# Projecting the recurrence values with 512 tokens moving, and turning them with VectorE blocks, in a hybrid decoder layer

## The chip, the cores and the metric

The kernel runs on one core of one Trainium2 chip. The metric is the device time of one execution in microseconds; a profiled execution also has a span, from its first to its last instruction, and a trace of every instruction and transfer. The engines are called PE or TensorE (matmul), PEld (its weight load), DVE or VectorE, ACT or ScalarE, POOL or GpSimd, and SP or SyncE, which here issues nearly all DMAs.

## The reference, cut to what matters

A decoder layer on 2048 tokens of width 1024 in float32. Its input projection feeds two groups of heads side by side: four recurrent heads (HGRN2) of width 128, and eight attention heads over a window of 128 tokens. The change is about `hi`, the values of the recurrent heads.

```python
u = rmsnorm(h, norm_mix_w[l])
proj = u @ w_in[l]
hq, hf, hi, hg, att = jnp.split(proj, [...], axis=-1)
f = lb + (1.0 - lb) * jax.nn.sigmoid(hf)
log_f, k_hg = jnp.log(f), 1.0 - f
q_hg = hq * (HG_DK ** -0.5)
v_hg = hi.reshape(B, S, HG_HEADS, HG_DV)
o_hg = hgrn2_chunkwise(q_hg, k_hg, v_hg, log_f)   # S_t = diag(f_t) S_{t-1} + k_t v_t^T,  o_t = S_t^T q_t
o_hg = rmsnorm(o_hg, hg_norm_w[l]) * silu(hg)
o_att = sliding_window_attention_with_sinks(...)
h = h + concatenate([o_hg, o_att]) @ w_out[l]
v = rmsnorm(h, norm_ffn_w[l])
h = h + (silu(causal_depthwise_conv(v @ w_gate[l])) * (v @ w_up[l])) @ w_down[l]
return rmsnorm(h, final_norm_w)
```

## The kernel before

The tokens are done in two halves of 1024. In each half there is a mixing stage (all head projections, the recurrence and the attention), then the output projection, gate and up projections, and the down projection. The normalized input X of a half lies in SBUF with the features on the partitions, as 8 pairs of tiles XH and XL, each 128 x 1024. Each float32 product is made of three matmuls in a faster format, from a high and a low part of either side (hi and lo of a weight, made by `prep` at L199 and L200; XH and XL of the input): XH x hi, XL x hi, XH x lo.

Most projections go through `unit` (L218): for one head, the weight tile of 128 x 128 is the stationary operand and 512 tokens move, so the result lies with the head's 128 columns on the partitions and the tokens along the row, in two PSUM tiles of 128 x 512, one for each 512 tokens: 8 x 3 x 2 = 48 matmuls. PSUM has eight banks of this size: four of kind mm, which the units use in turn, two of kind hg and two of kind at.

The values are needed the other way round, with tokens on the partitions. `project_v` (L670 to L686) therefore makes them with X as the stationary operand and the weights of two heads, 256 columns, moving: for each of the 8 groups of 128 tokens one mm bank `pvv`, filled by 24 matmuls of 256 columns (L681 to L683) and emptied by two ScalarE activations (L685), one for each head, which multiply by the token's norm `rs` as they copy. It is called twice in a half, once for heads 0 and 1 and once for heads 2 and 3. The values are read by `pu` (L614, with the transposed keys Kn, for the state's updates) and by `po` (L634, with the score tile ST).

What has a tile with tokens and columns exchanged elsewhere uses one of two ways: TensorE transposes through PSUM (`pkn` at L607 for the keys, `ppt`, `pot`), or the helper `turned` (L335): one VectorE instruction STREAM_TRANSPOSE (L338) exchanges rows and columns within each block of 32 x 32 into a tile `turn`, and sixteen DMAs on SyncE's queue (L341) carry the blocks, 32 KB a time and from SBUF to SBUF, to their places in the destination. The attention probabilities of head pairs 0 to 2 (`pt`, from `sc`) and the output of recurrent heads 0 to 2 (`hg`, from `on`) go that way. The tiles of tag pp, three buffers, serve both `turn` and the attention's `qx` (the split queries, L401 to L404) and `po` (the masked probabilities, L453).

The attention of one pair of heads j has these steps: `qa` projects the queries; `sc` makes, for each of two groups of 512 tokens, the scores `psc` (L414), the softmax on VectorE and ScalarE (maximum at L426, exponentials at L436, scaling at L441), and the turning into `pt`; `pv` and `pw` multiply with the values: `poT` (L471), from `pt` and from `po`. A recurrent head has the steps f, q (projections), l (seven levels of short matmuls `plev`, L558 and L572, with VectorE multiplications between them), s (keys transposed, `pu`, the states `SS`) and p (`po`, L634 and L639, and the norm). The string ORDER gives the order in which the steps are written out; the framework's scheduler then places every instruction in its engine's queue, mixing steps where their data allow, and each engine executes its queue in that order.

Of the kernel before, what the change touches and what calls it, by code (L numbers as in the profile page):

```python
# [36 lines left out]
            ("P7", "S3", "T3"), ("P2", "A12", "B21"), ("P4", "A22", "T4")]  # L37
AFTER = {2: 'po'}
UP_AFTER = 'T2'
ORDER = ("f0 q0 l0 qa0 v0 sc0 s0 p0 f1 q1 pv0 pw0 l1 qa1 sc1 f2 s1 p1 q2 pv1 pw1 l2 qa2 v1 sc2 f3 s2 p2 q3 pv2 "  # L40
         "pw2 l3 qa3 sc3 s3 p3 pv3 pw3 g0 g1 m4 m5 m6 g2 m0 m1 g3 m7 m2 m3").split()
LEVELS = [1, 2, 4, 8, 16, 32, 64]
NEG = -1.0e30
UT = 7
# [1 line left out]
VB = 2  # L46
TURNED_PAIRS = 3
TURNED_HEADS = 3


@with_exitstack
def hymba_layer(ctx: ExitStack, tc: tile.TileContext, a: dict, out: bass.AP, rows_out: bass.AP):
# [282 lines left out]
    def turned(p, tag, bufs, src, dst):  # L335

        t = p.tile([P, 4, 8, 32], F32, tag=tag, name="turn", bufs=bufs)
        nc.vector.transpose(t, src.rearrange("p n (c j) -> p c n j", j=32))  # L338
        for a in range(4):
            for c in range(4):  # L340
                nc.sync.dma_start(dst[32 * c:32 * c + 32, a], t[32 * a:32 * a + 32, c])  # L341

    def rows(kv):
        return slice(kv * HD, (kv + 1) * HD)
# [38 lines left out]
    def attend(hf, j, X, invb, KS, V, VD, mix, p):  # L383
# [9 lines left out]
        for g in range(NB):  # L393
            sc = p.tile([P, 2, 4, P], F32, tag="sc", name="sc", bufs=2)
            gs = slice(g * 512, (g + 1) * 512)
            for kv in range(2):
                r, other = rows(kv), rows(1 - kv)

                qx = p.tile([P, 2, 512], F32R, tag="pp", name="qx", bufs=3)
                qh, ql = qx[:, 0], qx[:, 1]  # L400
                nc.scalar.copy(qh[r], qT[r, gs])  # L401
                nc.scalar.copy(qh[other], qT[r, gs])
                nc.vector.tensor_tensor(ql[r], qT[r, gs], qh[r].bitcast(F32), op=ALU.subtract)
                nc.scalar.copy(ql[other], ql[r].bitcast(F32))  # L404
                for i0 in (0, 2):
                    pb = ps("at", "psc")
                    first = hf == 0 and g == 0 and i0 == 0
                    for i in range(2):
                        n = g * 4 + i0 + i
                        w0 = 1 if first and i == 0 else 0  # L410
                        o = pb[:, i * 256 + w0 * P:(i + 1) * 256]
                        ks = slice((n + w0) * P, (n + 2) * P)
                        for t, qx in enumerate((qh, ql)):
                            nc.tensor.matmul(o, qx[:, (i0 + i) * P:(i0 + i + 1) * P], KS[:, kv, ks],  # L414
                                             start=t == 0, stop=t == 1)
                    pv = pb.rearrange("p (i w k) -> p i w k", i=2, w=2)
                    dst = sc[:, kv, i0:i0 + 2]
                    if first:
                        nc.vector.memset(dst[:, 0], NEG)
                        nc.scalar.copy(dst[:, 1], pv[:, 1, 0])  # L420
                    else:
                        nc.scalar.copy(dst, pv[:, :, 0])
                    nc.vector.copy_predicated(
                        dst, C.own.bitcast(U32).unsqueeze(1).to_broadcast([P, 2, P]), pv[:, :, 1])
            m = p.tile([P, 2, 4], F32, tag="mx", name="m", bufs=2)
            nc.vector.tensor_reduce(m.rearrange("p a b -> p (a b)"),  # L426
                                    sc.rearrange("p a b c -> p (a b) c"), axis=AX.X, op=ALU.max)
# [4 lines left out]
            nc.vector.tensor_scalar(m, m, -1.0, None, op0=ALU.mult)
            den = p.tile([P, 2, 4], F32, tag="den", name="den", bufs=2)
            for kv in range(2):
                for i in range(4):
                    nc.scalar.activation(sc[:, kv, i], sc[:, kv, i], AF.Exp, bias=m[:, kv, i:i + 1],  # L436
                                         accum_out=den[:, kv, i:i + 1])
# [3 lines left out]
            nc.vector.tensor_tensor(sc, sc, den.unsqueeze(3).to_broadcast([P, 2, 4, P]), op=ALU.mult)  # L441
            if j < TURNED_PAIRS:
                pt = p.tile([P, 4, 8, 32], F32, tag="sc", name="pt", bufs=2)
                turned(p, "pp", 3, sc.rearrange("p a b c -> p (a b) c"), pt)
                sc = pt
            scs.append(sc)
        yield
# [37 lines left out]
    def hgrn(hf, h, X, invb, vs, WG, gates, mix, p, fu=None):  # L485
# [112 lines left out]
        v = vs[h]  # L598

        kept = TT if hf + 1 < NH else TT - 1  # L600
        Kn = p.tile([P, TT, P], F32, tag="t4", name="Kn", bufs=2)
        for b in range(NB):
            pk = ps("hg", "pkn")
            n = min(4, kept - 4 * b)
            for i in range(n):
                c = slice((b * 4 + i) * P, (b * 4 + i + 1) * P)
                nc.tensor.transpose(pk[:, i * P:(i + 1) * P], K[:, c], ident)  # L607
            nc.scalar.copy(Kn[:, 4 * b:4 * b + n].rearrange("p a b -> p (a b)"), pk[:, 0:n * P])
        SS = p.tile([P, TT, P], F32, tag="SS", name="SS", bufs=1)
        for b in range(NB):  # L610
            pu = ps("hg", "pu")
            for c in range(4 * b, min(4 * b + 4, kept)):
                i = c % 4
                marks["pu"] = nc.tensor.matmul(pu[:, i * P:(i + 1) * P], Kn[:, c], v[:, c], start=True, stop=True)  # L614
            for c in range(4 * b, min(4 * b + 4, kept)):
                i = c % 4
                if hf == 0 and c == 0:
                    nc.vector.tensor_copy(SS[:, 0], pu[:, 0:P])
                    continue
# [9 lines left out]
        for b in range(NB):  # L629
            at = [po[b][:, i * P:(i + 1) * P] for i in range(4)]  # L630
            empty = hf == 0 and b == 0
            for i in range(4):
                for k in range(2):
                    marks["po"] = nc.tensor.matmul(at[i][rows(k)], ST[:, k, 4 * b + i], v[:, 4 * b + i],  # L634
                                                   start=i == 0, stop=empty and i == 0, skip_group_check=True)
            for i in range(4):
                c = 4 * b + i
# [11 lines left out]
            mix[h] = g  # L649
        nc.vector.tensor_tensor(on, on, rs.unsqueeze(2).to_broadcast([P, TT, P]), op=ALU.mult)  # L650
        if h < TURNED_HEADS:
            turned(p, "t4", 2, on, q.rearrange("p (a c q) -> p a c q", a=4, c=TT))
        for b, bs in halves() if h >= TURNED_HEADS else ():
            pt = ps("hg", "pot")
            for i in range(4):
# [11 lines left out]
            nc.vector.tensor_copy(state[:, h], SS[:, TT - 1])  # L667
        yield

    def project_v(hf, pr, X, rs, p):  # L670

        v = [p.tile([P, TT, P], F32, tag="v", name="v", bufs=VB) for _ in range(2)]
        parts = [prep(a["w_v"][pr, s]) for s in range(2)]
        for tt in range(TT):
            o = ps("mm", "pvv")
            t = slice(tt * P, (tt + 1) * P)
            for kt in range(KT):
                hi, lo = parts[kt // 4]
                xh, xl = X[kt]
                c = slice((kt % 4) * 256, (kt % 4 + 1) * 256)  # L680
                nc.tensor.matmul(o[:, 0:256], xh[:, t], hi[:, c], start=kt == 0, stop=False)  # L681
                nc.tensor.matmul(o[:, 0:256], xl[:, t], hi[:, c], start=False, stop=False)  # L682
                nc.tensor.matmul(o[:, 0:256], xh[:, t], lo[:, c], start=False, stop=kt == KT - 1)  # L683
            for i in range(2):
                nc.scalar.activation(v[i][:, tt], o[:, i * P:(i + 1) * P], AF.Identity, scale=rs[:, tt:tt + 1])  # L685
# [468 lines left out]
    for hf in range(NH):  # L1154
        X, kv, invb, rs, f0 = nxt
        with ExitStack() as st:
# [7 lines left out]
            for name in ORDER:  # L1164
# [7 lines left out]
                elif stage == "w":  # L1172
                    WG[n] = prep(a["w_g"][n])
                elif stage == "v":
                    vs += project_v(hf, n, X, rs, p)
                else:
                    M[n] = split(mix[n], C.hgw if n < TURNED_HEADS else None)
            for n in (7, 3):
# [8 lines left out]
def _layout(i):  # L1187
# [3 lines left out]
    def cols(w, idx):  # L1191
# [10 lines left out]
    rows = [ar(P) + h * P for h in range(4)]  # L1202
    rows += [512 + np.concatenate([j * HD + ar(HD), (j + 4) * HD + ar(HD)]) for j in range(4)]
    w_out = i["w_out"][0][np.concatenate(rows)]
    w_v = np.stack([cols(w_in, 1024 + pr * 256 + ar(256)).reshape(P, 2, D).transpose(1, 0, 2) for pr in range(2)])
    conv = np.concatenate([i["conv_w"][0], i["conv_b"]], 0)
    d = {
        "xT": x.T.reshape(KT, P, S),
# [1 line left out]
        "norm_mix_w": i["norm_mix_w"][0].reshape(KT, P).T,  # L1210
        "w_q": np.stack([cols(w_in, h * P + ar(P)) for h in range(4)]),
        "w_f": np.stack([cols(w_in, 512 + h * P + ar(P)) for h in range(4)]),
        "w_v": w_v,
        "w_g": np.stack([cols(w_in, 1536 + h * P + ar(P)) for h in range(4)]),
        "w_att": np.stack([cols(w_in, c) for c in att]),
        "b_attn": np.stack([b[c - att0] for c in att], 1),
# [37 lines left out]
```

## Time and profile before

| what | value |
|---|---|
| runs, median of three | 2129.17 us (2129.09 to 2129.24) |
| the profiled execution | 2129.44 us |
| its span | 2127.7 us |
| mean granted TensorE clock | 0.999 |
| PE busy | 2113.7 us (99%) |
| VectorE busy | 1632.4 us (77%) |
| ScalarE busy | 1050.0 us (49%) |
| mixing stage of half 0, roughly | 45 to 346 us |
| mixing stage of half 1, roughly | 1085 to 1400 us |

A row of the timeline reads: start, duration, engine, line, operation, tile written, tile read, count, and in brackets the idle time before it with what ended it. A row of a group ends in busy time, mean ns of one, and the idle time before its members. A row of a stretch has its bounds, its length, then for each engine the busy time and the count, the granted clock, the DMA share and GB/s. Matmuls overlap: the duration of one is longer than the distance between the starts of two.

### The profile page before, as it was taken

What the parts mean: (1) busy time and instruction counts of PE and PEld (TensorE: products, weight loads), DVE (VectorE), ACT (ScalarE), POOL (GpSimd) and SP (SyncE); (2) the same over time, 40 slices, a digit from 0 to 9 for tenths busy, and PEclk for the clock granted to TensorE, in tenths of its full rate; (3) what the DMA queues carried; (4) which work ended last, traced back from release to release, by engine and by line L of the source; (5) the groups of instructions that cost most, each with busy time, mean ns of one, the idle gap of its engine ahead of it and who ended that gap; (6) DMA issues with size and microseconds to landing.
All of it is one profiled execution on the core that took longest, in us unless ns stands there. A gap on an engine that the chain in (4) does not pass through costs nothing.

```text
span 2127.7 us, 30275 instructions
## 1 busy us (share of the span) xinstructions
PE 2113.7 (99%) x11575; PEld 1763.0 (83%) x11575; DVE 1632.4 (77%) x2427; ACT 1050.0 (49%) x1855; POOL 16.9 (1%) x43
## 2 busy tenths in 40 slices
PE   8999999999999999999999999999999999999998
PEld 6988888888888888888889898888888888888887
DVE  6587786798887878785865776867988788887765
ACT  5455645564444445335635456555544444453353
POOL 2000000000000000000000000000000000000000
PEclk9999999999999999999999999999999999999999
DMA  4121213413232335964641212242223323259644
GB/s 162 42 59 45 68 52 102 136 59 121 91 124 92 98 116 168 379 235 150 216 143 40 61 38 64 60 146 97 80 99 103 110 90 124 94 194 403 228 149 134
DMA packets 105810, 264.34 MB, mean 124 GB/s; under 512 B 15808, under 2 KB 28608, under 8 KB 105664
## 3 DMA queue, kind: packets, MB, share of 16 engines
q1 hardware_dynamic: 105232, 262.14, 36.6%
q8 instruction: 91, 1.49, 0.3%
q14 instruction: 55, 0.45, 0.1%
q10 hardware_dynamic: 432, 0.27, 0.0%
HBM read 195.56 MB, written 57.34 MB: 119 GB/s over the span
## 4 chain that ended last, share of the span: by engine, by line
PE 97%; DVE 2%; DMA 1%; ACT 0%; issue 0%; SPq 0%; ACTq 0%; DVEq 0%
PE X L818 7%; PE X L816 7%; PE X L817 7%; PE pop L218 7%; PE hq L218 4%; PE q L218 4%; PE g L218 4%; PE f L218 4%; PE Y L817 4%; PE Y L818 4%; PE Y L816 4%; PE pdx L1004 3%; PE pdx L1003 3%; PE pdx L1005 3%; PE pdy L1004 3%; PE pdy L1003 3%
## 5 line engine op out<-in xcount | busy, mean ns | idle before, releaser
L689 ACT CAST whi<-raw 128x1024 fp32r<-128x1024 f32 x88 | 92.7, 1053 | 115.1 <-PE X L817 73.1
L816 PE MATMUL X<-T,whi 128*128 128x512 f32 x352 | 136.9, 389 | 0.0
L817 PE MATMUL X<-T,whi 128*128 128x512 f32 x352 | 136.9, 389 | 0.0
L818 PE MATMUL X<-T,wlo 128*128 128x512 f32 x352 | 136.9, 389 | 0.0
L887 DVE SCALAR_TENSOR_TENSOR y<-ga,cw,y 128x1024 f32<-128x1024 f32 x88 | 112.5, 1279 | 25.9 <-ACT y L885 25.9
L822 ACT COPY u<-X 128x512 f32<-128x512 f32 x88 | 51.5, 585 | 122.8 <-PE X L818 122.6
L690 DVE TENSOR_TENSOR wlo<-raw,whi 128x1024 fp32r<-128x1024 f32 x88 | 107.2, 1218 | 4.4 <-ACT whi L689 4.4
L199 ACT CAST whi<-raw 128x1024 fp32r<-128x1024 f32 x58 | 60.6, 1050 | 89.9 <-PE pop L218 36.7
L690 DVE TENSOR_TENSOR xld<-raw,xhd 128x1024 fp32r<-128x1024 f32 x72 | 80.9, 1131 | 18.3 <-ACT xhd L689 18.2
L689 ACT CAST xhd<-raw 128x1024 fp32r<-128x1024 f32 x72 | 70.0, 978 | 37.6 <-DMA raw<-act0T 12.0
L218 PE MATMUL pop<-XL,whi 128*128 128x512 f32 x256 | 82.8, 390 | 0.0
L218 PE MATMUL pop<-XH,wlo 128*128 128x512 f32 x256 | 82.6, 390 | 0.0
L218 PE MATMUL pop<-XH,whi 128*128 128x512 f32 x256 | 82.5, 391 | 0.0
L200 DVE TENSOR_TENSOR wlo<-raw,whi 128x1024 fp32r<-128x1024 f32 x58 | 70.5, 1217 | 10.4 <-ACT whi L199 10.1
L818 PEld LDWEIGHTS X<-T,wlo 128*128 128x128 f32 x352 | 66.1, 188 | 13.8
L817 PEld LDWEIGHTS X<-T,whi 128*128 128x128 f32 x352 | 66.1, 188 | 13.7
L816 PEld LDWEIGHTS X<-T,whi 128*128 128x128 f32 x352 | 66.0, 188 | 13.7
L682 PE MATMUL pvv<-whi,XL 128*128 128x256 f32 x256 | 72.7, 285 | 0.0
L681 PE MATMUL pvv<-whi,XH 128*128 128x256 f32 x256 | 72.6, 285 | 0.0
L683 PE MATMUL pvv<-wlo,XH 128*128 128x256 f32 x256 | 72.4, 287 | 0.0
L818 PE MATMUL X<-B,wlo 128*128 128x512 f32 x176 | 68.7, 390 | 0.8 <-DVE wlo L690 0.8
L817 PE MATMUL X<-T,Sh 128*128 128x512 f32 x176 | 68.6, 390 | 0.5 <-DVE T L690 0.5
(388 smaller groups left out, 6287.9 us busy)
## 6 DMA issues: line engine op xcount, KB each, us to landing
wr<-in_w_down SPq DMA_DIRECT2D x90, 512.0 KB, 5.6
raw<-in_w_gate SPq DMA_DIRECT2D x44, 512.0 KB, 3.6
raw<-in_w_up SPq DMA_DIRECT2D x44, 512.0 KB, 3.6
raw<-act0T SPq DMA_DIRECT2D x20, 512.0 KB, 5.6
raw<-act1T SPq DMA_DIRECT2D x20, 512.0 KB, 5.9
act0B<-y SPq DMA_DIRECT2D x33, 256.0 KB, 2.4
act1B<-y SPq DMA_DIRECT2D x33, 256.0 KB, 2.4
raw<-in_w_out SPq DMA_DIRECT2D x16, 512.0 KB, 3.7
```

Source lines behind the costliest of these rows:

```text
L218: nc.tensor.matmul(o[b], w, x[:, bs], start=f, stop=l)
L681: nc.tensor.matmul(o[:, 0:256], xh[:, t], hi[:, c], start=kt == 0, stop=False)
L682: nc.tensor.matmul(o[:, 0:256], xl[:, t], hi[:, c], start=False, stop=False)
L683: nc.tensor.matmul(o[:, 0:256], xh[:, t], lo[:, c], start=False, stop=kt == KT - 1)
L689: nc.scalar.copy(h, src)
L690: return (eng or nc.vector).tensor_tensor(l, src, h.bitcast(F32), op=ALU.subtract)
L816: nc.tensor.matmul(o, wh[:, ws], xh, start=i == 0 and not more, stop=False, skip_group_check=more)
L817: nc.tensor.matmul(o, wh[:, ws], xl, start=False, stop=False, skip_group_check=more)
L818: nc.tensor.matmul(o, wl[:, ws], xh, start=False, stop=i == 3, skip_group_check=more)
L887: nc.vector.scalar_tensor_tensor(y, g[:, w:w + HALF], C.cw[:, ft, w:w + 1], y, op0=ALU.mult, op1=ALU.add)
L1003: nc.tensor.matmul(o, wh[:, i, c], ah[:, i, cols], start=f, stop=False, skip_group_check=more)
L1004: nc.tensor.matmul(o, wh[:, i, c], al[:, i, cols], start=False, stop=False, skip_group_check=more)
```

## The change

The values of each head are projected by `unit`, with the weights stationary and 512 tokens moving, into two PSUM tiles `vT0` and `vT1`. The helper `turned`, which now takes a list of sources, transposes them in blocks of 32 x 32, with one VectorE instruction for each PSUM tile, into `turn`, and its sixteen DMAs carry the blocks into the tile `v`, now laid out as 4 strips of 32 columns for each group of 128 tokens. ScalarE then multiplies each group of 128 tokens by its norm in place. The step v stands for one head instead of two; in ORDER v0 v1 stand where v0 stood, and v2 v3 where v1 stood. TURNED_KEYS is 0, so the keys go through `pkn` as before. The DMAs in `turned` are the same as before, from `turn` to the destination.

```diff
-ORDER = ("f0 q0 l0 qa0 v0 sc0 s0 p0 f1 q1 pv0 pw0 l1 qa1 sc1 f2 s1 p1 q2 pv1 pw1 l2 qa2 v1 sc2 f3 s2 p2 q3 pv2 "
+ORDER = ("f0 q0 l0 qa0 v0 v1 sc0 s0 p0 f1 q1 pv0 pw0 l1 qa1 sc1 f2 s1 p1 q2 pv1 pw1 l2 qa2 v2 v3 sc2 f3 s2 p2 ...
+TURNED_KEYS = 0
 def turned(p, tag, bufs, src, dst):
     t = p.tile([P, 4, 8, 32], F32, tag=tag, name="turn", bufs=bufs)
-    nc.vector.transpose(t, src.rearrange("p n (c j) -> p c n j", j=32))
+    for i, s in enumerate(src):
+        n = 8 // len(src)
+        nc.vector.transpose(t[:, :, i * n:(i + 1) * n], s.rearrange("p (n c j) -> p c n j", n=n, j=32))
     for a in range(4):
         for c in range(4):
             nc.sync.dma_start(dst[32 * c:32 * c + 32, a], t[32 * a:32 * a + 32, c])
...
-                marks["pu"] = nc.tensor.matmul(pu[:, i * P:(i + 1) * P], Kn[:, c], v[:, c], start=True, stop=True)
+                marks["pu"] = nc.tensor.matmul(pu[:, i * P:(i + 1) * P], Kn[:, :, c] if h < TURNED_KEYS else Kn[:, c], v[:, :, c], start=True, stop=True)
...
-                    marks["po"] = nc.tensor.matmul(at[i][rows(k)], ST[:, k, 4 * b + i], v[:, 4 * b + i],
+                    marks["po"] = nc.tensor.matmul(at[i][rows(k)], ST[:, k, 4 * b + i], v[:, :, 4 * b + i],
...
-    def project_v(hf, pr, X, rs, p):
-        v = [p.tile([P, TT, P], F32, tag="v", name="v", bufs=VB) for _ in range(2)]
-        parts = [prep(a["w_v"][pr, s]) for s in range(2)]
-        for tt in range(TT):
-            o = ps("mm", "pvv")
-            t = slice(tt * P, (tt + 1) * P)
-            for kt in range(KT):
-                ...
-                nc.tensor.matmul(o[:, 0:256], xh[:, t], hi[:, c], start=kt == 0, stop=False)
-                nc.tensor.matmul(o[:, 0:256], xl[:, t], hi[:, c], start=False, stop=False)
-                nc.tensor.matmul(o[:, 0:256], xh[:, t], lo[:, c], start=False, stop=kt == KT - 1)
-            for i in range(2):
-                nc.scalar.activation(v[i][:, tt], o[:, i * P:(i + 1) * P], AF.Identity, scale=rs[:, tt:tt + 1])
+    def project_v(h, X, rs, p):
+        o = unit(a["w_v"][h], X, "vT")
+        v = p.tile([P, 4, TT, 32], F32, tag="v", name="v", bufs=VB)
+        turned(p, "pp", 3, o, v)
+        for c in range(TT):
+            nc.scalar.activation(v[:, :, c], v[:, :, c], AF.Identity, scale=rs[:, c:c + 1])
         return v
```

The scheduler's order moves with it. Three places matter for what follows, all in half 0. On TensorE, the end of the second values pass before the change: the last pvv matmuls, the first two poT of the second group of pair 1 (they read pt, which the sixteen DMAs fill), a level plev, the rest of poT, and the first matmuls of f of head 3.

```order
L681 MATMUL pvv<-whi,XH 128x256
L682 MATMUL pvv<-whi,XL 128x256
L471 MATMUL poT<-pt,V 64x128 [waits DMAHW4_49,DMAHW5_49,DMAHW3_49,DMAHW6_49,DMAHW2_49,DMAHW7_49,DMAHW1_49,DMAHW0_49]
L471 MATMUL poT<-pt,V 64x128
L558 MATMUL plev<-Q,G 64x2x32 [waits DVE_49,Activation_49]
L558 MATMUL plev<-Q,G 64x2x32 x7
L683 MATMUL pvv<-wlo,XH 128x256
L414 MATMUL psc<-KS,qx 128x128 [waits Activation_49]
L471 MATMUL poT<-po,VD 64x128 [waits DVE_49]
```

The same place after the change, from the last level of 16 on, which now follows the end of the last vT unit and the first group's poT: three levels, the transposes of K (pkn) and poT of the second group stand behind each other, and f of head 3 comes after them.

```order
L560 MATMUL plev<-Q,G 64x2x32 x7
L574 MATMUL plev<-Q,K 32x32 [waits DVE_49]
L574 MATMUL plev<-Q,K 32x32 x15
L574 MATMUL plev<-Q,K 64x64 [waits DVE_49,PE_49]
L574 MATMUL plev<-Q,K 64x64 x7
L613 MATMUL pkn<-ident,K 128x128 [waits DVE_49,PE_49,Activation_49]
L613 MATMUL pkn<-ident,K 128x128 x3
L613 MATMUL pkn<-ident,K 128x128 [waits PE_49,Activation_49]
L613 MATMUL pkn<-ident,K 128x128 x3
L473 MATMUL poT<-pt,V 64x128 [waits DMAHW4_49,DMAHW5_49,DMAHW3_49,DMAHW6_49,DMAHW2_49,DMAHW7_49,DMAHW1_49,DMAHW0_49]
```

Before, matmuls of pvv stood between the levels and up to poT; now no vT or f matmul stands between the last two levels, pkn and this poT. The third place is on VectorE, after the change: the multiplications of the last two levels, the masked probabilities po of pair 1's second group, which wait for the DMAs of pt, then the four block transposes of v2 (vT_2182 and vT_2183) and v3 (vT_2266 and vT_2267), and a qx of pair 2.

```order
L577 TENSOR_TENSOR Q<-Q,F_2073 128x16x32 [waits DVE_49,PE_49]
L578 TENSOR_TENSOR K<-K,F_2073 128x16x32
L577 TENSOR_TENSOR Q<-Q,F_2096 128x8x64 [waits DVE_49,PE_49]
L578 TENSOR_TENSOR K<-K,F_2096 128x8x64 [waits DVE_49]
L455 TENSOR_TENSOR po<-pt,ownT 128x1024 [waits DMAHW4_49,DMAHW5_49,DMAHW3_49,DMAHW6_49,DMAHW2_49,DMAHW7_49,DMAHW1_49,DMAHW0_49]
L340 STREAM_TRANSPOSE turn<-vT_2182 128x4x128
L340 STREAM_TRANSPOSE turn<-vT_2183 128x4x128
L340 STREAM_TRANSPOSE turn<-vT_2266 128x4x128
L340 STREAM_TRANSPOSE turn<-vT_2267 128x4x128
L405 TENSOR_TENSOR qx<-att_2171,qx 64x512 [waits PE_49,Activation_49]
```

The transposes are new on VectorE, and they stand directly behind that po. Half 1 has the same sequence at all three places, except that one level of 16 more stands there without matmuls of vT or f ahead of poT.

More of the change, by code (lines that the diff above doesn't have):

```diff
@@ L39 @@
 UP_AFTER = 'T2'
-ORDER = ("f0 q0 l0 qa0 v0 sc0 s0 p0 f1 q1 pv0 pw0 l1 qa1 sc1 f2 s1 p1 q2 pv1 pw1 l2 qa2 v1 sc2 f3 s2 p2 q3 pv2 "
-         "pw2 l3 qa3 sc3 s3 p3 pv3 pw3 g0 g1 m4 m5 m6 g2 m0 m1 g3 m7 m2 m3").split()
+ORDER = ("f0 q0 l0 qa0 v0 v1 sc0 s0 p0 f1 q1 pv0 pw0 l1 qa1 sc1 f2 s1 p1 q2 pv1 pw1 l2 qa2 v2 v3 sc2 f3 s2 p2 q3 pv2 pw2 l3 qa3 sc3 s3 p3 pv3 pw3 g0 g1 m4 m5 m6 g2 m0 m1 g3 m7 m2 m3").split()
 LEVELS = [1, 2, 4, 8, 16, 32, 64]
@@ L443, in attend @@
                 pt = p.tile([P, 4, 8, 32], F32, tag="sc", name="pt", bufs=2)
-                turned(p, "pp", 3, sc.rearrange("p a b c -> p (a b) c"), pt)
+                turned(p, "pp", 3, [sc.rearrange("p a b c -> p (a b c)")], pt)
                 sc = pt
@@ L600, in hgrn @@
         kept = TT if hf + 1 < NH else TT - 1
-        Kn = p.tile([P, TT, P], F32, tag="t4", name="Kn", bufs=2)
-        for b in range(NB):
+        if h < TURNED_KEYS:
+            Kn = p.tile([P, 4, TT, 32], F32, tag="t4", name="Kn", bufs=2)
+            turned(p, "pp", 3, [K], Kn)
+        else:
+            Kn = p.tile([P, TT, P], F32, tag="t4", name="Kn", bufs=2)
+        for b in range(NB) if h >= TURNED_KEYS else ():
             pk = ps("hg", "pkn")
@@ L651, in hgrn @@
         if h < TURNED_HEADS:
-            turned(p, "t4", 2, on, q.rearrange("p (a c q) -> p a c q", a=4, c=TT))
+            turned(p, "t4", 2, [on.rearrange("p c t -> p (c t)")], q.rearrange("p (a c q) -> p a c q", a=4, c=TT))
         for b, bs in halves() if h >= TURNED_HEADS else ():
@@ L668, in hgrn @@
         yield
-    def project_v(hf, pr, X, rs, p):
-        v = [p.tile([P, TT, P], F32, tag="v", name="v", bufs=VB) for _ in range(2)]
-        parts = [prep(a["w_v"][pr, s]) for s in range(2)]
-        for tt in range(TT):
-            o = ps("mm", "pvv")
-            t = slice(tt * P, (tt + 1) * P)
-            for kt in range(KT):
-                hi, lo = parts[kt // 4]
-                xh, xl = X[kt]
-                c = slice((kt % 4) * 256, (kt % 4 + 1) * 256)
-                nc.tensor.matmul(o[:, 0:256], xh[:, t], hi[:, c], start=kt == 0, stop=False)
-                nc.tensor.matmul(o[:, 0:256], xl[:, t], hi[:, c], start=False, stop=False)
-                nc.tensor.matmul(o[:, 0:256], xh[:, t], lo[:, c], start=False, stop=kt == KT - 1)
-            for i in range(2):
-                nc.scalar.activation(v[i][:, tt], o[:, i * P:(i + 1) * P], AF.Identity, scale=rs[:, tt:tt + 1])
+    def project_v(h, X, rs, p):
[4 more added lines that the diff above has]
+            nc.scalar.activation(v[:, :, c], v[:, :, c], AF.Identity, scale=rs[:, c:c + 1])
         return v
@@ L1174, in hymba_layer @@
                 elif stage == "v":
-                    vs += project_v(hf, n, X, rs, p)
+                    vs.append(project_v(n, X, rs, p))
                 else:
@@ L1204, in _layout @@
     w_out = i["w_out"][0][np.concatenate(rows)]
-    w_v = np.stack([cols(w_in, 1024 + pr * 256 + ar(256)).reshape(P, 2, D).transpose(1, 0, 2) for pr in range(2)])
     conv = np.concatenate([i["conv_w"][0], i["conv_b"]], 0)
@@ L1212, in _layout @@
         "w_f": np.stack([cols(w_in, 512 + h * P + ar(P)) for h in range(4)]),
-        "w_v": w_v,
+        "w_v": np.stack([cols(w_in, 1024 + h * P + ar(P)) for h in range(4)]),
         "w_g": np.stack([cols(w_in, 1536 + h * P + ar(P)) for h in range(4)]),
```

## The prediction

> **What bounds the kernel now.** First the page's head and its chain of waits, to see which engine sets the end:
>
> ```profile
> span 2127.7 us, 30275 instructions
> ...
> PE 2113.7 (99%) x11575; PEld 1763.0 (83%) x11575; DVE 1632.4 (77%) x2427; ACT 1050.0 (49%) x1855; POOL 16.9 (1%) x43
> ...
> PE 97%; DVE 2%; DMA 1%; ACT 0%; issue 0%; SPq 0%; ACTq 0%; DVEq 0%
> ```
>
> TensorE is the bound: 99% busy and 97% of the chain. Next, all waits of TensorE (us in total, times, longest), since a busy share of 99% could still hide small gaps:
>
> ```profile
> PE kv L218 <- ACT XH L232: 5.5, 1, 5.5
> PE X L818 <- DVE wlo L690: 0.8, 2, 0.4
> PE X L817 <- DVE T L690: 0.5, 1, 0.5
> PE kv L218 <- DVE XL L233: 0.3, 1, 0.3
> PE poT L471 <- DVE po L463: 0.2, 1, 0.2
> ```
>
> Apart from the 5.5 us at the start, all waits together are 1.8 us. So the time is the sum of TensorE's start-to-start intervals: work taken off TensorE comes off the span one for one, and every idle microsecond put into TensorE's order is added one for one. Both occur here.
>
> **TensorE work removed and added.** Two rows from the stretches of the tile pvv and of g (one 512-wide gate unit per head), then one from an unbroken stretch of the output projection, then two neighbouring matmuls from the timeline:
>
> ```profile
> sum 650.00, PE 99.26 PEld 93.98 ACT 19.75; mean PE 7.64 PEld 7.23 ACT 1.52
> ```
> ```profile
> 40.00:420.00 380.00, 46.57 (x192) 35.39 (x192) 5.38 (x8) 1.00 0.23 69
> ```
> ```profile
> 360.00:415.00 55.00, 55.00 (x244) 45.53 (x244) 7.68 (x12) 1.00 0.40 134
> ```
> ```profile
> 72.00 0.28 PE L682 MATMUL pvv<-whi,XL 128*128 128x256 f32 x1
> 72.12 0.28 PE L683 MATMUL pvv<-wlo,XH 128*128 128x256 f32 x1
> ```
>
> All 768 pvv matmuls (4 passes of 192, 256 wide) hold TensorE for 99.26 us. Their place is taken by 8 units of 48 matmuls of 512. Four g units, broken up by other work as the new ones are, take 46.57 us, so eight take 93.1: **6.2 us saved**. Undisturbed intervals say nearly the same: 768 x 0.120 = 92.2 against 384 x 55.00/244 (0.2254) = 86.6, 5.6 saved. Twice the width costs 1.88 times, not 2, because something like 13 ns per matmul does not shrink with it. The ends are 4 and 7 us; I take 6.2, from units cut up alike.
>
> [...]
>
> **What is free, and by what cover.** The values are now read by pu and po in four strips of 32 columns. poT already reads a tile in that layout (pt) and one that is not (po):
>
> ```profile
> L471 PE MATMUL poT<-po,VD 128*64 128x128 f32 x128 | 12.8, 278 | 0.0
> ...
> L471 PE MATMUL poT<-pt,V 128*64 128x128 f32 x84 | 8.3, 276 | 0.0
> ```
>
> 278 and 276 ns: nothing. ScalarE's 64 evacuations of pvv become 64 scalings of the same size: nothing while its 49% stays off the path. VectorE gains 16 block transposes of 128x512, SyncE 128 copies of 32 KB. Their prices stand in these rows (a group's mean ns of one, then the timeline, then the landing time of the line that issues the copies):
>
> ```profile
> L388 DVE SCALAR_TENSOR_TENSOR att<-q,invb 128x512 f32<-128x512 f32 x8 | 5.1, 682 | 0.6 <-PE q L218 0.6
> ```
> ```profile
> 208.57 1.24 DVE L338 STREAM_TRANSPOSE turn<-sc 128x1024 f32<-128x1024 f32 x1
> ...
> 222.35 1.23 DVE L453 TENSOR_TENSOR po<-pt,ownT 128x1024 f32<-128x1024 f32 x1
> ```
> ```profile
> 209.89 10.84 SPq L341 DMA_DIRECT2D pt<-turn  x16
> ```
> ```profile
> 1268.80 10.01 SPq L341 DMA_DIRECT2D pt<-turn  x16
> ```
> ```profile
> DMA to landing us min/median/max: 1.8/1.8/3.6
> ```
>
> A transpose of half the size out of PSUM is between 0.62 (half of 1.24) and 0.68 (the PSUM read at L388); I take 0.65, 10.4 us in all, hidden where VectorE has slack. Each turned head holds SyncE's queue for 10.0 to 10.8 us, 40 to 43 us per half. The queue rows of the new order put loads of later weights behind v0 and v1, but some 35 us of TensorE's rows lie between such a load and its first matmul: hidden, at about 11 us each if that cover went. Nothing goes through DRAM: the helper turned still issues sixteen copies from the turn tile straight into its destination, so the words "1 write, 4 reads" describe no part of this code.
>
> **The wait that is added.** A pvv tile held one mm bank for 24 matmuls (2.9 us) and ScalarE emptied it at once. A vT unit holds two of the four mm banks for 48 matmuls until VectorE has transposed both. In the rows of the new order, the transposes of v2 and v3 stand on VectorE behind the second po of pair 1, which waits for the sixteen copies of pt. Queued behind that po are both heads' transposes and qx of pair 2; f of head 3 needs their banks. On TensorE itself poT, ahead of f, waits for the same copies. So TensorE runs into the softmax of pair 1: scores (psc), softmax, transpose, sixteen copies, poT. In the kernel before that chain was covered:
>
> ```profile
> 197.28 1.14 PE psc L414 x8
> ...
> 225.03 1.68 PE poT L471 x28
> ...
> 1250.80 1.15 PE psc L414 x8
> ...
> 1283.42 1.68 PE poT L471 x28
> ```
> ```profile
> 1281.18 1.22 DVE L453 TENSOR_TENSOR po<-pt,ownT 128x1024 f32<-128x1024 f32 x1 [1.06 <-DMA hg<-turn]
> ```
>
> Half 0: the last score ends at 198.4, the copies are issued from 209.89 to 220.7 and land by about 222 (po at 222.35 did not wait): 24 us. Half 1: 1252.0 to 1281.18, where po did wait 1.06 us: 29 us. Between the same points the new order leaves TensorE this much, by the rows of one level's matmuls and of the transposes of K:
>
> ```profile
> 69.37 0.69 PE L558 MATMUL plev<-Q,G 128*64 128x64 f32 x16
> ```
> ```profile
> 241.28 0.87 PE pkn L607 x8
> ```
>
> Half 0: 53 vT matmuls x 0.2254 = 11.9, about 3.6 levels x 0.69 = 2.5, the two last levels 1.4, pkn 0.87, the first poT 1.7: 18.4 us. Half 1: 59 vT 13.3, five levels 3.5, the 32-wide level 0.75, the first poT 1.7, the rest of po and pdiag 1.6: 20.8 us. That leaves idle 5.6 to 10.8 us in half 0 and 3.1 to 8.4 in half 1. f then needs po (1.2) and two transposes (1.3) after the landing, against the 1.7 that poT takes meanwhile: 0.8 more each. Together 10 to 21 us; I take **15**, the middle, since each half showed its own end of the chain and the new order keeps neither exactly.
>
> The same chain is shorter at v0: the second qx of pair 0 waits for v0's copies, and the scores stand about 18.3 us of matmuls behind v0, against 1.3 for the transposes, 10.0 to 10.8 of issue, 1.8 to land, and ScalarE's scaling and qx. The row for the scaling:
>
> ```profile
> L685 ACT ACTIVATE v<-pvv,y 128x128 f32<-128x128 f32 x32 | 9.8, 361 | 14.7 <-PE pvv L683 14.5
> ```
>
> Eight of these are 2.5 to 2.9, the qx steps about 2: 18 to 19 us in all, so 0 to 2 us; I take 1 for the kernel. Later users of v0 to v3 come when the copies are 1 us or more past.
>
> **The sum.** -6.2 + 15 + 1 = +9.8 us. The profiled execution took 2129.44 us, its span 2127.7; the runs' median is 2129.17, 0.3 lower, and I apply the difference to the median: **2139.0 us**. By the bounds: -7 + 10 + 0 = +3, and -4 + 21 + 2 = +19, so 2132 to 2148 for this case. A measurement of this kernel can tell about 0.2% (4.3 us) from no change.
>
> **Rivals.** *Faster: the copies land before TensorE needs them.* The pieces of the softmax alone are shorter than the 11.5 us that passed between scores and copies:
>
> ```profile
> L436 ACT ACTIVATE sc<-sc,m 128x128 f32<-128x128 f32 x64 | 24.8, 389 | 0.2 <-DVE m L432 0.2
> ...
> L441 DVE TENSOR_TENSOR sc<-sc,den 128x1024 f32<-128x1024 f32 x8 | 9.8, 1220 | 0.1
> L426 DVE TENSOR_REDUCE m<-sc 128x8 f32<-128x1024 f32 x8 | 9.7, 1215 | 0.1
> ```
>
> Eight exponentials 3.1, reduction 1.2, scaling 1.2, transpose 1.2, copies and small steps 1.8: 8.5, with 10.0 and 1.8 behind it 20.3 us. If VectorE and ScalarE serve this chain ahead of the rest, half 1 is covered and half 0 lacks 2 us. It decides below about 2 us of idle in all: 2123 to 2125 us, I say 2123.5. Against it: VectorE executes its rows in order with levels and weight splits between those steps, as before. Chance 0.15.
>
> *About even.* The chain takes some 21 to 22 us, idle 5 to 8 us, which eats the saving: 2130 us. Chance 0.20.
>
> *The clock falls.* At the start, before TensorE had been busy for long, its 512-wide matmuls started 0.43 us apart, and in the last window, after its work ended, the granted clock averages 0.77:
>
> ```profile
> 7.67 0.63 PE L218 MATMUL kv<-XL,whi 128*128 128x512 f32 x1
> 8.10 0.63 PE L218 MATMUL kv<-XH,wlo 128*128 128x512 f32 x1
> ```
> ```profile
> 2120.00:2127.70 7.70, 1.13 (x6) 0.77 0.35 111
> ```
>
> If each long idle stretch puts TensorE back there for as long as the start lasted (5.5 to 11.3 us, 13 matmuls that would need 2.9 us), each half loses 2.8 us more: 2139.0 + 5.6 = 2144.6 us. Against it: small matmuls (levels, pkn) break the idle into pieces of about 3 us. Chance 0.12. [...]
>
> **How the numbers follow.** The forecast has 0.53, the fall of the clock 0.12 (both slower by over 0.2%), about even 0.20 (within 0.2%), covered 0.15 (faster). The forecast's own range is 2132 to 2148; reaching down to the even case and most of the covered one gives 2124 to 2148, which leaves out some 0.1 at each end.
>
> **What would show it.** Right: no pvv; 384 vT matmuls at 0.225 to 0.243 us; TensorE waits of 4 to 11 us in each half at the second poT of pair 1 and at the f behind it, put down to the copies of pt or to VectorE's turn; nothing elsewhere over 2 us. Wrong: no such wait (then the saving stands), waits at pu for v's copies or for weight loads behind them on SyncE's queue (then the queue is the cost), vT intervals above 0.243, or a granted clock under 1.00 in the middle.

## The result, and the profile after

The changed kernel takes 2149.93 us (2147.33 to 2150.15) against 2129.20 us: a ratio of 1.0094, 95% interval 1.0077 to 1.0112, so 20.7 us slower. The prediction said 2139.0 us, 2124 to 2148. The profiled execution took 2150.09 us, its span is 2148.4 us.

The head of the page and the waits of TensorE (total, times, longest):

```profile
span 2148.4 us, 29717 instructions
PE 2119.7 (99%) x11191; PEld 1749.2 (81%) x11191; DVE 1638.2 (76%) x2443; ACT 1050.4 (49%) x1855; POOL 16.3 (1%) x43
```
```profile
PE poT L473 <- DVE po L465: 3.1, 2, 2.4
PE plev L560 <- DVE Q L567: 2.7, 1, 2.7
PE poT L473 <- DMA pt<-turn: 2.6, 3, 1.6
PE plev L574 <- DVE Q L567: 2.0, 2, 1.2
PE plev L574 <- DVE K L578: 1.7, 1, 1.7
PE pkn L613 <- DVE K L578: 1.5, 1, 1.5
PE poT L473 <- DVE po L455: 1.1, 2, 0.6
```

TensorE is still 99% busy, but waits that the kernel before did not have come to 14.6 us. All but 0.7 us of them stand at three places. The first is the second poT of pair 1 in half 0, in TensorE's timeline:

```profile
222.47 0.66 PE L560 MATMUL plev<-Q,G 128*64 128x64 f32 x16
224.32 0.70 PE L574 MATMUL plev<-Q,K 128*32 128x32 f32 x32 [1.18 <-DVE Q L567]
226.67 0.72 PE L574 MATMUL plev<-Q,K 128*64 128x64 f32 x16 [1.66 <-DVE K L578]
228.88 1.94 PE L613 MATMUL pkn<-ident,K 128*128 128x128 f32 x8 [1.48 <-DVE K L578]
232.42 0.69 PE L473 MATMUL poT<-pt,V 128*64 128x128 f32 x4 [1.60 <-DMA pt<-turn]
233.69 0.70 PE L473 MATMUL poT<-po,VD 128*64 128x128 f32 x4 [0.57 <-DVE po L455]
...
236.87 0.74 PE L218 MATMUL f<-XH,whi 128*128 128x512 f32 x1
```

1.18 + 1.66 + 1.48 + 1.60 + 0.57 = 6.5 us idle, and f of head 3 only after it. The first three of these pieces, 4.3 us, wait for VectorE's multiplications between the levels, and only 2.2 us are put down to the copies of pt and to po. The copies still set the end: po, on VectorE, has been waiting 3.68 us for them when it starts. VectorE at the same place shows why f could not come earlier: the transposes of v2 and v3, whose matmuls had ended by 220.7, stand behind po.

```profile
232.41 1.23 DVE L455 TENSOR_TENSOR po<-pt,ownT 128x1024 f32<-128x1024 f32 x1 [3.68 <-DMA pt<-turn]
233.66 2.51 DVE L340 STREAM_TRANSPOSE turn<-vT 128x512 f32<-128x512 f32 x4
```

Half 1 has the same stall, 2.67 + 0.79 + 0.34 + 0.56 = 4.4 us, with 3.5 us of it at the levels. Here one level more stands ahead of poT, and the last level and pkn come only behind the start of f.

```profile
1292.34 1.12 PE L560 MATMUL plev<-Q,G 128*64 128x64 f32 x16 [2.67 <-DVE Q L567]
1294.25 1.07 PE L574 MATMUL plev<-Q,K 128*32 128x32 f32 x32 [0.79 <-DVE Q L567]
1295.66 0.69 PE L473 MATMUL poT<-pt,V 128*64 128x128 f32 x4 [0.34 <-DMA pt<-turn]
1296.92 0.69 PE L473 MATMUL poT<-po,VD 128*64 128x128 f32 x4 [0.56 <-DVE po L455]
```

The last scores of pair 1 stand in these two rows, so from their end to poT it is 26.2 us in half 0 and 26.8 us in half 1:

```profile
205.48 0.74 PE L416 MATMUL psc<-KS,qx 128*128 128x256 f32 x4
...
1267.69 1.20 PE L416 MATMUL psc<-KS,qx 128*128 128x256 f32 x8
```

The third place is one that the prediction did not name: the end of half 0, where the probabilities of pair 3 are transposed (ppt) and multiplied, with 2.42 + 0.67 = 3.1 us idle. At the end of half 1 it is 0.7.

```profile
365.55 0.44 PE L473 MATMUL poT<-pw,V 128*64 128x128 f32 x4 [2.42 <-DVE po L465]
366.66 0.44 PE L473 MATMUL poT<-po,VD 128*64 128x128 f32 x4 [0.67 <-DVE po L465]
```

Now the granted clock, the third number from the end of each row, in stretches of half 0, of the end of half 0 and of half 1 (ahead of it stand the busy times and counts of PE, PEld, VectorE, ScalarE and GpSimd):

```profile
223.00:227.50 4.50, 1.56 (x53) 1.16 (x48) 3.50 (x9) 1.08 (x4) 0.00 (x0) 0.96 0.21 51
227.50:233.50 6.00, 2.63 (x12) 1.89 (x12) 2.32 (x3) 1.84 (x4) 0.00 (x0) 0.50 0.41 117
233.50:237.50 4.00, 3.81 (x30) 3.40 (x31) 2.64 (x5) 0.51 (x2) 0.00 (x0) 0.51 0.08 19
237.50:242.00 4.50, 4.50 (x22) 3.72 (x21) 0.69 (x1) 1.83 (x4) 0.00 (x0) 1.00 0.21 53
```
```profile
367.00:370.50 3.50, 3.50 (x29) 2.98 (x26) 0.00 (x0) 0.93 (x2) 0.00 (x0) 0.52 0.00 0
```
```profile
1292.00:1297.00 5.00, 2.97 (x54) 2.28 (x56) 3.96 (x8) 0.72 (x2) 0.00 (x0) 0.51 0.21 54
1297.00:1302.50 5.50, 5.50 (x34) 4.70 (x35) 4.29 (x7) 2.15 (x4) 0.00 (x0) 0.51 0.19 48
```

Each stall ends in matmuls at half rate (0.50 to 0.52 in these rows): pkn takes 1.94 us instead of 0.87. Half of the busy time in the rows at 0.50 to 0.52 is put down to the clock: (2.63 + 3.81) / 2 = 3.2, 3.50 / 2 = 1.8 and (2.97 + 5.50) / 2 = 4.2, together 9.2 us. This is bookkeeping, not what a full clock would give back: pkn's extra 1.1 us, and 0.8 us at two levels of half 1, stand ahead of the landing of the copies, where TensorE would otherwise have waited as much longer.

The account: if each interval from the start of a TensorE instruction to the next start is put down to its tile, the values take 92.0 us (384 vT) instead of 96.4 (768 pvv). -4.4 + 14.6 idle + 9.2 at half rate = +19.4; the spans differ by 20.7. The 1.3 us left over are many small intervals.

### The profile page after: what moved, and what is told of

Its sections match the earlier page's. It is cut to its first block, busy times and chain, and to the rows that moved or that the text cites. A ratio compares the mean times of both kernels' runs of the same rounds, so it can differ in the third digit from the quotient of the medians.

```text
span 2148.4 us, 29717 instructions
## 1 busy us (share of the span) xinstructions
PE 2119.7 (99%) x11191; PEld 1749.2 (81%) x11191; DVE 1638.2 (76%) x2443; ACT 1050.4 (49%) x1855; POOL 16.3 (1%) x43
## 4 chain that ended last, share of the span: by engine, by line
PE 94%; DVE 3%; SPq 1%; DMA 1%; ACT 1%; issue 0%; DVEq 0%; ACTq 0%
PE pop L218 7%; PE X L815 7%; PE X L814 7%; PE X L813 7%; PE q L218 4%; PE g L218 4%; PE f L218 4%; PE hq L218 4%; PE Y L814 4%; PE Y L813 4%; PE Y L815 4%; PE pdx L1000 3%; PE pdx L1002 3%; PE pdx L1001 3%; PE vT L218 3%; PE pdy L1000 3%
## 5 line engine op out<-in xcount | busy, mean ns | idle before, releaser
L814 PEld LDWEIGHTS X<-T,whi 128*128 128x128 f32 x352 | 66.1, 188 | 13.7
L815 PEld LDWEIGHTS X<-T,wlo 128*128 128x128 f32 x352 | 66.1, 188 | 13.7
L813 PEld LDWEIGHTS X<-T,whi 128*128 128x128 f32 x352 | 66.1, 188 | 13.7
L813 PE MATMUL Z<-B,whi 128*128 128x512 f32 x176 | 68.7, 391 | 0.0
L813 PE MATMUL X<-B,whi 128*128 128x512 f32 x176 | 68.7, 390 | 0.0
L815 PE MATMUL Z<-B,wlo 128*128 128x512 f32 x176 | 68.6, 390 | 0.0
```

The source lines that it names most:

```text
L813: nc.tensor.matmul(o, wh[:, ws], xh, start=i == 0 and not more, stop=False, skip_group_check=more)
L814: nc.tensor.matmul(o, wh[:, ws], xl, start=False, stop=False, skip_group_check=more)
L815: nc.tensor.matmul(o, wl[:, ws], xh, start=False, stop=i == 3, skip_group_check=more)
```

## The experiments

After this trace there were two theories of the added wait. Mine: v2 and v3 hold the mm banks until they are turned (bank theory), later sharpened: they are turned late because their tile turn waits for one of the three buffers of tag pp (slot theory). The rival: each turned head costs, for its copies and transposes (queue theory). Every run was timed against the kernel before on the same chip; ratios are to it. The diffs of all but the ninth start from the changed kernel.

**1. Only heads 0 and 1 changed.** Heads 2 and 3 go through pvv, which ScalarE writes into the strips (the function `old_v`, the step v3 taken out of ORDER and the weights' layout are left out of the lines below).

```diff
-                    vs.append(project_v(n, X, rs, p))
+                    vs += old_v(1, X, rs, p) if n == 2 else [project_v(n, X, rs, p)]
```

> Only v0 and v1 are projected by vT units and turned; heads 2 and 3 go through pvv as before, with ScalarE writing the strips. In the trace of the changed kernel the values took 92.0 us of TensorE's start-to-start time instead of 96.4, and three places lost the rest: about 10 us at the second poT of pair 1 in half 0, about 9 in half 1, about 6 at the end of half 0 (idle time and half-rate matmuls together). Bank theory (mine): the first two losses come from v2 and v3 holding the mm banks until VectorE turns them; with pvv there they go. 2129.2 - 2.2 = 2127.0 us, TensorE waits under 2 us at that poT. Queue theory (rival): each turned head costs for its sixteen copies and its transposes, wherever it stands; half of the heads, half of the loss: 2129.2 - 2.2 + 12.5 = 2139.5 us, with waits near v0 and v1.

Measured 2129.96 us, ratio 1.0002 (0.9993 to 1.0011), clock 0.999, no wait over 0.5 us in the mixing stages. The two turned heads cost no stall, which speaks against the queue theory. Of the expected 2.2 us of gain none is left: ppt and the levels took 1.1 us more each, in small pieces.

**2. Only heads 2 and 3 changed**, the same edit for the other pair.

> Only v2 and v3 are projected by vT units and turned; heads 0 and 1 go through pvv. Bank theory: both losses at the second poT of pair 1 stay, 10 and 9 us, and the saving is half: 2129.2 - 2.2 + 19 = 2146 us, or 2152 if the end of half 0 loses its 6 us too. Queue theory: 2139.5 us, as with the other pair.

Measured 2140.04 us, ratio 1.0048 (1.0036 to 1.0061). The stall at the second poT of pair 1 is there in both halves, with a granted clock of 0.50 behind it; all waits there come to 9 us. In time alone this is the queue theory's number, 2139.5 us. But that theory forecast as much for the other pair, which lost nothing, and the loss stands at the place that the bank theory names. Of the 19 us expected there, it made about 13: the 9 us and 4 us at half rate; the end of half 0 lost 0.2 us.

**3. The matmuls without the turn.**

```diff
-        turned(p, "pp", 3, o, v)
-        for c in range(TT):
-            nc.scalar.activation(v[:, :, c], v[:, :, c], AF.Identity, scale=rs[:, c:c + 1])
+        for c in range(TT):
+            oc = o[c // 4].rearrange("p (c a q) -> p c a q", c=4, a=4)[:, c % 4]
+            nc.scalar.activation(v[:, :, c], oc, AF.Identity, scale=rs[:, c:c + 1])
```

> The matmuls alone: vT units as in the changed kernel, but ScalarE copies each block of 128 columns from PSUM straight into v, without the exchange of rows and columns and without its copies, so the values stand the wrong way round. Bank theory: ScalarE frees the banks at once, f can fill the stretch; what is left is the saving alone, 4.4 us by the intervals in the trace of the changed kernel (my prediction said 6.2): 2124.8 us, clock 0.999. Filler theory (rival): a unit of 48 matmuls of 512 is used up sooner than 192 of 256 in eight banks, so the stretch is bare in any case: above 2140 us with the turn left out too.

Measured 2129.67 us, ratio 1.0000 (0.9991 to 1.0009). No wait at the second poT of pair 1: the stall came from the turn, not from the coarser units. But the saving is gone again, at one place, the end of half 0, where TensorE waits for pair 3 and the mean granted clock of the stretch is 0.89:

```profile
PE poT L473 <- ACT pw L464: 1.9, 1, 1.9
PE po L640 <- DVE m L434: 1.4, 1, 1.4
```
```profile
345.00:360.00 15.00, 11.30 (x123) 9.82 (x122) 10.34 (x33) 9.64 (x41) 0.00 (x0) 0.89 0.01 2
```

So the third place of the changed kernel needs no turn to lose time.

**4. The turn in another buffer.**

```diff
-        turned(p, "pp", 3, o, v)
+        turned(p, "t4", 2, o, v)
```

> The tile turn of the values is taken from the two buffers of tag t4 (shared with Kn and on) instead of the three of tag pp (shared with qx and po); matmuls, transposes and copies are all the same. Slot theory (a sharper form of mine): v2 and v3 are turned late because pp has no free buffer until po of pair 1 has been read, and po waits for the copies of pt; with another tag they are turned when their matmuls end, the banks come free and f fills the stretch: 2129.2 - 4.4 = 2125 us, up to 2129 if t4 makes a smaller wait of its own. Queue theory: the same number of transposes and copies, so about 2150 us again.

Measured 2126.30 us, ratio 0.9986 (0.9978 to 0.9995): 23 us taken off the changed kernel by one tag, and 0.14% faster than the kernel before. The same transposes and copies are made, so the queue theory is out. Around the place of the stall in half 0 TensorE is never idle and its clock stays whole:

```profile
195.00:245.00 50.00, 50.00 (x421) 40.82 (x420) 38.85 (x77) 25.63 (x79) 0.00 (x0) 1.00 0.16 39
```

**5. The banks freed by ScalarE, the turn in pp.**

```diff
-        turned(p, "pp", 3, o, v)
+        e = v.rearrange("p a c q -> p (a c q)")
+        for b, bs in halves():
+            nc.scalar.copy(e[:, bs], o[b])
+        turned(p, "pp", 3, [e], v)
```

> ScalarE copies each vT bank into v as it stands (16 copies of 128x512 more, about 0.59 us each by the copy of poT in the trace), VectorE transposes from there into turn, still a buffer of pp, and the sixteen copies write v back. Bank theory: f needs only the banks, and those are free 1.2 us after the unit; f stands between the levels in the rows, no wait of TensorE over 2 us at the second poT of pair 1: 2125 to 2128 us although turn waits for pp as before. If the late buffer of pp itself were the cost (values late for pu, or qx of pair 2 behind the turn), waits at pu or psc of 5 us and more in each half: over 2139 us.

Measured 2151.76 us, ratio 1.0113 (1.0099 to 1.0127): nothing gained, and over 2139 us as the second forecast has it. Its waits are not at pu or psc, though. The stall at pair 1 is gone in both halves, as the bank theory says (first row, half 0), but the loss has moved to the ends of the halves (the other two):

```profile
205.00:250.00 45.00, 45.00 (x353) 35.45 (x350) 37.34 (x71) 18.65 (x48) 0.00 (x0) 1.00 0.17 45
...
345.00:363.00 18.00, 13.17 (x135) 11.29 (x132) 14.93 (x38) 11.22 (x45) 0.00 (x0) 0.91 0.00 1
...
1413.00:1436.00 23.00, 14.22 (x105) 11.72 (x104) 12.93 (x29) 11.18 (x40) 0.00 (x0) 0.70 0.05 11
```

With free banks TensorE does f and g earlier; the attention is late, and where it falls due there is no other work left. The last scores of pair 3 start at 347 and 1417 us, against 339 and 1403 in the changed kernel and 321 and 1389 in the fourth run. So the banks decide where TensorE waits; whether they also cost time in all, this run cannot say, since its sixteen copies may cost time of their own (eleventh run).

**6. TensorE kept busy through the stall.**

```diff
+            for _ in range(({16: 8, 32: 12, 64: 24}, {8: 20, 16: 6, 32: 4})[hf].get(m, 0) if h == 2 else 0):
+                nc.tensor.matmul(pl[:, 256:512], X[0][0][:, 0:P], X[0][0][:, 0:256], start=True, stop=True)
```

> The changed kernel with 74 matmuls of 256 columns more, whose result nobody reads, in unused columns of the levels' PSUM banks of head 2: 44 in half 0, 30 in half 1, at 0.120 us each 5.3 and 3.6 us, where TensorE stood idle for 6.5 and 4.4 us. Clock theory: the idle time is filled and nothing waits longer, and the matmuls behind it (pkn, poT, first f) run at full rate: 3.3 and 4.4 us come back, about 2142 us, with no stretch under 1.00 around the second poT of pair 1. Idle theory (rival: the loss is the waiting alone, the granted clock changes nothing that counts): 2150 us or 1 to 3 us more.

Measured 2140.26 us, ratio 1.0055 (1.0042 to 1.0069): 74 matmuls more, and 8 us less than the changed kernel. The clock stays at 1.00 where it was 0.50:

```profile
227.50:233.50 6.00, 5.09 (x55) 4.45 (x55) 3.15 (x5) 1.91 (x4) 0.00 (x0) 1.00 0.40 117
```

The half rate can be read apart from the waits behind the landing of the copies, from the first poT that reads po to the first f. The same 28 matmuls stand there in both kernels:

```profile
232.32 0.44 PE L473 MATMUL poT<-po,VD 128*64 128x128 f32 x4 [0.51 <-DVE po L455]
...
234.00 0.50 PE L218 MATMUL f<-XH,whi 128*128 128x512 f32 x1
```

That is 1.68 us here and 3.18 in the changed kernel (233.69 to 236.87), and half 1 gives the same two numbers. These 1.5 us in each half, with 0.2 and 1.0 us at f itself, make 4.2 us that come back at the two places, not 7.7: some of the added matmuls delayed pkn and poT, and some of the half rate stood where TensorE had to wait in any case. Most of the rest of the 8 us stands at the end of half 0, where the order of the rows is another and no wait is left. So the half rate is a cost of its own, but a smaller one than the bookkeeping has.

**7. Through DRAM: one write and four reads for each turned tile.**

```diff
-        for a in range(4):
-            for c in range(4):
-                nc.sync.dma_start(dst[32 * c:32 * c + 32, a], t[32 * a:32 * a + 32, c])
+        d = dp.tile([P, 4, 256], F32, tag="td", name="td", bufs=4)
+        nc.sync.dma_start(d, t.rearrange("p c n q -> p c (n q)"))
+        for a in range(4):
+            nc.sync.dma_start(dst[:, a], d[32 * a:32 * a + 32].rearrange("i c (n q) -> c i n q", q=32))
```

> What the few words on the change say, and its code does not do: every turned tile (values, pt, hg) goes to DRAM in one write of 512 KB and comes back in four reads of 128 KB, 5 DMAs instead of 16. In the trace of the changed kernel the sixteen hold SyncE for 10.0 us and the last lands some 2 to 3 us later. Chain theory: the stall is the chain that ends in these copies; five issues take about 3 us and two trips some 2 to 4 us each, 7 to 11 us in all instead of 12 to 13, so the idle time falls by 2 to 5 us in each half: 2135 to 2145 us, lower if vT or f stands in the bare stretch. Rival: the second trip costs more than the eleven issues saved, chain and stall grow: over 2150 us.

Measured 2186.94 us, ratio 1.0271 (1.0257 to 1.0285): a miss of both forecasts' sizes, on the rival's side.

```profile
PE poT L474 <- DMA pt<-td: 23.5, 6, 6.0
PE psc L417 <- DVE sc L426: 11.1, 4, 5.5
```

At pair 1 in half 0 it is 12.0 us from the end of the transpose (223.56) to po (235.58), against 12.9 with sixteen copies (219.55 to 232.41): five issues take less of the queue (0.33 + 2.27 = 2.6 us against 10.0), but the two trips take back nearly all of it: the reads are issued 2.3 us after the write, and po starts 7.1 us after the last issue instead of 2.8. At the second po of every turned pair, six in the two halves, it is alike: 10.9 to 13.0 us against 11.6 to 13.3 with sixteen copies. So a longer way of pt does not explain the 37 us. TensorE waits longer (the rows above), its mean granted clock is 0.989, in the changed kernel 0.994, and the scheduler's order differs; what cost the 37 us stays open.

**8. v3 written out later**, behind pw2.

> Only the string of steps: v3 is written out behind pw2 instead of behind v2, so that two banks, not four, hang on the transposes behind the second po of pair 1. All the work is the same. Bank theory: f and hq of head 3 find two free banks and fill the stretch: 2125 to 2128 us. Chain theory (rival: the chain from the scores of pair 1 to its poT is simply longer now, whatever holds the banks): waits of 4 to 6 us at that poT stay, above 2140 us.

Measured 2139.49 us, ratio 1.0049 (1.0036 to 1.0061). Two free banks did what the bank theory says at pair 1 and gained half of the loss only: the wait at its poT is gone, but g waits 2.3 and 1.5 us for VectorE, behind the longer of these waits the granted clock is 0.50, and at the end of half 0 poT of pair 3 waits twice for 1.0 us. Part of the loss moved again; the bank theory alone does not give the time.

**9. The kernel before, with two buffers of pp.** `bufs=3` of tag pp becomes 2 in all its places.

> The kernel before, with pvv and no turned values, but with two buffers of tag pp instead of three: the suspected cause alone. Slot theory: the values' turn costs the attention a buffer of pp; taking one away without any turned value must do the same: the scores of pair 3 end later than at 316 us of half 0, ppt and poT of pair 3 stand at the end of each half without pop between them, and 5 to 12 us are lost, 2134 to 2141 us. Bank theory or queue theory: nothing that they name has changed, 2129 us, at most 2131.

Measured 2133.72 us, ratio 1.0021 (1.0013 to 1.0030): 4.4 us slower without any turned value, a little less than the low end. The last scores of pair 3 start at 343 us instead of 316, and TensorE waits 1.1 us in each half at the second poT of pair 1, the place of the changed kernel's stall. A buffer of pp is worth that much to the attention alone.

**10. The other buffer, and qa3 sc3 ahead of l3.**

> The turn in tag t4 as in the run with the other buffer, and in the string of steps qa3 sc3 stand ahead of l3, so that the last softmax starts earlier. In the run with the other buffer 2.8 us were left at the transposes ppt at the ends of the halves. If these are what remains of the loss: 2126.3 - 2.8 = 2123.5 us. Rival: the levels of head 3 are late instead, po and pot wait by as much: 2126 us or more.

Measured 2129.33 us, ratio 1.0001 (0.9992 to 1.0010). ppt lost 2.3 us less, but pop, the levels and the scores took it back: the rival was right.

**11. The other buffer, and the banks freed by ScalarE.**

> The turn in tag t4, and the vT banks emptied by ScalarE into v first: both the buffer of pp and the banks are free at once. If the banks cost anything beside the buffer, it is faster than the run with the other buffer (2126.3), down to 2124; if the buffer was all, the same or up to 3 us slower, for 16 copies of 0.59 us more on ScalarE.

Measured 2137.57 us, ratio 1.0039 (1.0026 to 1.0052), 11 us above the fourth run, more than either forecast. The longest waits are again at the ends of the halves. ScalarE's sixteen copies, and transposes that read SBUF, are the only difference, so the fifth run is not a clean measure of the banks: part of its loss may be theirs. How they delay the attention was not found.

**12. Only v2 and v3 in the other buffer.**

```diff
-        turned(p, "pp", 3, o, v)
+        turned(p, *(("pp", 3) if h < 2 else ("t4", 2)), o, v)
```

> The turns of v2 and v3 alone are in tag t4; v0 and v1 stay in pp. TensorE's rows are those of the changed kernel word for word up to the first vT unit of head 3, 25 matmuls into it; from there f of head 3 stands between the last levels and ahead of the second poT of pair 1, in both halves. Slot theory: the stall at that poT (6.5 and 4.4 us idle, and 3 to 4.5 us of half-rate matmuls each) was made by the buffer of pp that v2 and v3 wait for, and by nothing that happened earlier: no wait over 1 us there, clock 1.00, 2149.9 - 19 = 2131 us, some 3 us less or more by what the end of half 0 still loses. Rival: v0 and v1 in pp had already put the attention behind (its scores of pair 1 end at 206 us as in the changed kernel, 193 with all turns in t4), and the wait stays or moves to a later pair: above 2140 us.

Measured 2132.71 us, ratio 1.0020 (1.0011 to 1.0029). The transposes on VectorE in half 0 now come soon after the units end, 23 us earlier for v2 and 14 for v3 than in the changed kernel, and ahead of both po:

```profile
210.25 1.31 DVE L340 STREAM_TRANSPOSE turn<-vT 128x512 f32<-128x512 f32 x2
221.29 1.31 DVE L340 STREAM_TRANSPOSE turn<-vT 128x512 f32<-128x512 f32 x2
...
226.27 1.18 DVE L455 TENSOR_TENSOR po<-pt,ownT 128x1024 f32<-128x1024 f32 x1
```
```profile
220.00:244.00 24.00, 24.00 (x204) 19.14 (x203) 17.78 (x30) 10.91 (x20) 0.00 (x0) 1.00 0.19 49
1262.00:1292.00 30.00, 28.36 (x251) 22.20 (x252) 25.38 (x48) 12.35 (x33) 0.00 (x0) 1.00 0.18 48
```

TensorE's rows in half 0 are those of the changed kernel into the unit of v3, at 218.4 us, and the scores of pair 1 end at 206 us in both: what came earlier did not make the stall. In half 1 the transposes are 18 us earlier for v2 and 3.5 for v3, and one wait over 1 us is left that the forecast had ruled out: f waits 1.6 us for the transposes of v2 (the second row). The buffer that v2 and v3 share with the attention made the stall, and it is worth 16 (by the ratios) to 17 (by the medians) of the 20.7 us. A fourth buffer of pp, which would have tested the same without touching t4, was not run.

## Why the prediction was wrong

- **The saving**, 6.2 us: 4.4 by start-to-start intervals, near the low end of the range. vT units are cut up more than those of g: the same 384 matmuls take 92.0 us there and 90.1 for g in this trace.
- **The added wait**, 15 us: right in its places and its chain, 6.5 + 4.4 = 10.9 us, near its lower bound of 10. In its form it was right in part: most of the idle time stands at the levels and pkn just ahead of poT, not at poT and f. From the end of the last score to poT it was 26.2 and 26.8 us, between the 24 and 29 taken; TensorE was busy about 2 us longer than reckoned, about half of it because pkn and the levels ran at half rate. The prediction put the transposes of v2 and v3 behind po and stopped there; the cause, that both wait for buffers of one tag, was in the text only as a remark that pp serves turn, qx and po. The twelfth run shows it. f did not wait behind poT: its transposes were covered.
- **v0's copies**, 1 us: 0, no wait at psc. The free edits stayed free: no wait for v's copies at pu, nor for weight loads behind them.
- With these the sum would have been -4.4 + 10.9 = +6.5 us. The step that failed is the one against a rival: "small matmuls (levels, pkn) break the idle into pieces of about 3 us". They do, into pieces of at most 2.7, and the clock fell to 0.50 all the same (that short pieces would spare it, no row of the kernel before had shown): 9.2 us by the bookkeeping, 7.4 of it at the two places of the forecast, where the sixth run got 4.2 us back. The prediction put this at nothing in the sum, as a rival with a chance of 0.12 and a price of 5.6 us. It was not a rival but a sequel of the forecast, and belonged in the sum; "a granted clock under 1.00 in the middle" stood among its own signs of being wrong.
- The second step that failed is "nothing elsewhere over 2 us": 3.1 us idle at the end of half 0 and 0.7 at the end of half 1. With the 1.8 us at half rate behind it, the end of half 0 comes to 4.9 us by the same bookkeeping. A later step of the attention falls due where TensorE has no other work. The third run loses time there too, without any turn, so no turn is needed for it; which row makes pair 3 late there stays open.
- "1 write, 4 reads" was read rightly as no part of the code; done in earnest it is 37 us slower still.

## What to carry to other kernels

When a new step borrows a buffer from a tag, list who else takes that tag and what each holder waits for: one tag here was worth 16 to 23 us, about four to five times the gain that the change was made of. When TensorE is the bound and every stall is made up of small waits, price the matmuls behind a stall at half rate as well: here waits of at most 2.7 us came with a granted clock of 0.50. And a wait that an edit removes in one place must be looked for at the end of the stage before it counts as gained.

## What the runs showed of the hardware

In the changed kernel the granted clock fell without one long idle stretch. It is at 0.50 in these three stretches, and at 1.00 between them:

```profile
227.18:237.42 10.24, 6.58 (x48) 5.29 (x44) 5.03 (x7) 2.33 (x5) 0.00 (x0) 0.50 0.28 78
367.13:370.54 3.41, 3.41 (x27) 2.89 (x24) 0.00 (x0) 0.97 (x2) 0.00 (x0) 0.50 0.00 0
1292.14:1302.38 10.24, 8.35 (x85) 6.88 (x86) 8.12 (x14) 2.75 (x6) 0.00 (x0) 0.50 0.20 51
```

It fell 2.5 to 4.1 us after TensorE's rows first became thin (at 223.1, 363.1 and 1289.7 us). In 223.0 to 227.5 TensorE was busy for 1.56 of 4.50 us, a third of the time, and no single wait in that stretch was over 1.7 us. It came back 3.7 to 5.5 us after work was continuous again (from 233.7, 366.7 and 1296.9 us). What decides whether it falls, these runs do not show.

The three stretches at half rate lasted 10.24, 3.41 and 10.24 us. By the granted clock in rows of 1 us, one lasted 3.4 us in the second run (226 to 230 us), one 3.4 us in the eighth (290 to 294) and one 13.7 us in the fifth (1421 to 1436).

The way of a turned tile pt, from the end of the transpose to its reader, was about as long through DRAM (10.9 to 13.0 us in the seventh run) as through sixteen copies (11.6 to 13.3 in the changed kernel), at six places each.
